# Hybrid decoder trunk: weights of the mixing projections split one step ahead across passes, channel pieces inside the u projection, a late pool stage, and key/value sums in two banks

## The chip, the cores and the metric

The kernel runs on one core of one Trainium2 chip. A core has a matrix engine (PE, which multiplies into eight PSUM banks of 128 x 512 float32), a vector engine (DVE), a scalar engine (ACT), a general engine (POOL), and a queue processor (SP) that here issues nearly all transfers between HBM and the on-chip memory. The metric is the device time of one execution in microseconds (us), the median of the runs shown.

## The reference

Two layers over a sequence of 1024 positions of width 1024, one batch, all in float32. Each layer first mixes tokens and then channels.

```python
h = rms_norm(x, g_pre_mix[l]) * (1.0 + scale_m) + shift_m
proj = h @ w_in[l] + b_in[l]                       # 1024 -> 1280
q, k, v, u = split(proj)                           # 512, 128, 128, 512
attn_out = sliding_window_attention_with_sinks(rotary(q), rotary(k), v, sinks[l])
pool_out = causal_pool_mixer(u, pool_w[l], pool_scale[l])
mix = concatenate([attn_out, pool_out], axis=-1) @ w_out[l]
x = x + gate_m * rms_norm(mix, g_post_mix[l])
h = rms_norm(x, g_pre_ffn[l]) * (1.0 + scale_f) + shift_f
f = (jax.nn.silu(h @ w_gate[l]) * (h @ w_up[l])) @ w_down[l]      # width 2816
x = x + gate_f * rms_norm(f, g_post_ffn[l])
```

Attention has 8 query heads on 2 key/value heads of width 64, a window of 128 and one learned sink per head. The pool mixer takes four groups of 128 channels of u, forms trailing means over 2, 4, 8 and 16 positions minus the token, and multiplies each group by its own 128 x 128 matrix. The six shifts, scales and gates of a layer come from a product of a conditioning vector with `ada_w`.

## The kernel before

**Precision.** Every matmul operand is split into a rounded part hi (ACT, line 213) and the rest lo (DVE, line 214), and each product is three matmuls: hi·hi, hi·lo, lo·hi (lines 239, 242 and 243, function `mm3`). `weight` (216) loads 128 x 512 weights into a staging part called raw and splits them. raw, hi and lo are rings of wide tiles that `part` (124) cuts into pieces of 512 columns: eight pieces of raw, six of hi and six of lo. A new wide tile is only handed out when everything that used the oldest one is done.

**Halves and passes.** The sequence is worked in two halves of 512 positions. The normalised, transposed activations of a half stand in eight tiles hT (one per 128 channels), each holding hi and lo. The input projection of a half is three passes, each over eight steps of 128 channels: `q_pass` (653; four banks of 128 positions x 512), `kv_pass` (617; four banks of which only 256 columns are used, weights of two steps loaded at once, so four steps to the outside), and `u_pass` (674; transposed, four banks of 128 channels x 512 positions). All take their banks from the tag acc, which has four; attention, transposes and the pool product share three banks of the tag msc, and attention's output has one, pv. At the end of a pass the banks are emptied: the query and key/value sums by DVE adds of the bias (lines 672 and 651), the u sums by ACT (line 686).

**Streams.** The passes, attention, the pool mixer and the `ada_w` sums ("side") are Python generators. `run` (596) steps one main stream and, after each of its steps, a share of the others. In a layer the order is: the queries and keys of half 0 (`dense0`, with side); then `dense`, which is u of half 0, keys/values of half 1, queries of half 1, with attention of half 0, the pool mixer of half 0 and side between its 20 steps; then the output projection of half 0 (`mix_out`) with side and attention of half 1; the post-norm of half 0; u of half 1 with ten steps of attention; the channel pieces of half 0 (line 1362); and then `firsts[0]`, the first six jobs of the up product (`up_firsts`, 1002), with the rest of attention and the pool mixer of half 1. A channel piece (`pre_norm_piece`, 494) is four transposes on PE into an msc bank, a scale and shift on ACT into raw (line 475), a store of that to HBM where it is kept for later (line 498), and a split into a tile of hT.

**Weights.** A pass calls `weight` at the start of each step, ahead of that step's matmuls. Only the first queries and keys of layer 0 already split the next step's weights ahead of the current step's matmuls (`first` and `pairs`).

**Order.** The library that turns this program into instructions plans the order on each engine: the order in which the program emits instructions is a priority, and one that is expected to be ready earlier can go out before one emitted ahead of it. Within an engine the instructions then run in the planned order, each waiting on semaphores for what it reads and for the buffer that it writes. This holds for SP's queue of transfers too.

Of the kernel before, what the change touches and what calls it, by code (L numbers as in the profile page):

```python
# [11 lines left out]
F32 = mybir.dt.float32  # L12
# [3 lines left out]
AF = mybir.ActivationFunctionType  # L16
# [49 lines left out]
def hybrid_decoder_kernel(  # L66
# [144 lines left out]
    def split(hi, lo, src):  # L211

        nc.scalar.activation(hi, src, AF.Copy)  # L213
        nc.vector.tensor_sub(lo, src, hi.bitcast(F32))  # L214

    def weight(*srcs):

        raw = part("raw")
        for psl, view, src in srcs:
            dst = raw[psl]  # L220
            if view:
                dst = dst.rearrange("p (a b) -> p a b", a=view)
            nc.sync.dma_start(dst, src)
        hi, lo = part("hi"), part("lo")
        split(hi, lo, raw)
        return hi, lo

    def after(ins, prev):
        tc.add_manual_dep(
            ins.ins, prev.ins.name,  # L230
            mybir.DependencyInfo(mybir.DependencyClass.NoSync, mybir.DependencyReason.DATA),
            reason="order on the same engine",
        )

    ALLP = slice(0, P)
    tiles = [slice(t * P, (t + 1) * P) for t in range(NT)]
# [377 lines left out]
    halos = {}  # L614
    attn = {}

    def kv_pass(l, hT, par, qkvs, pairs=None):

        if pairs:
            dsts = [pairs[t // 2][:, t % 2 * 256 : t % 2 * 256 + 256] for t in range(NT)]  # L620
        else:
            dsts = [acc_bank()[:, :256] for _ in range(NT)]

        def rows(k):
            return weight(
                (ALLP, 2, w_in[l, k * P : (k + 2) * P, ATT:QKV].rearrange("(a p) n -> p a n", p=P))
            )

        ahead = None
        if pairs:  # L630
            ahead = rows(0)
            yield
        for k in range(KD):
            if k % 2 == 0:
                (wh, wl), ahead = ahead or rows(k), None
            elif pairs and k + 1 < KD:
                ahead = rows(k + 1)
            cs = slice(k % 2 * 256, k % 2 * 256 + 256)
            hi, lo = hT[k]
            for t in range(NT):  # L640

                first, second = pairs and t % 2 == 0, pairs and t % 2 == 1
                other = mm3(
                    dsts[t], hi[:, tiles[t]], lo[:, tiles[t]], wh[:, cs], wl[:, cs],
                    k == 0 and not second, k == KD - 1 and not first,
                    other if second and k in (0, KD - 1) else None,
                )
            if k % 2 == 1:
                yield
        for t in range(NT):  # L650
            nc.vector.tensor_add(qkvs[t][:, ATT:QKV], dsts[t], par["bq"][:, ATT:QKV])

    def q_pass(l, hT, par, qkvs, first=False):

        banks = [acc_bank() for _ in range(NT)]

        def rows(k):
            return weight((ALLP, None, w_in[l, k * P : (k + 1) * P, 0:ATT]))

        ahead = None  # L660
        if first:
            ahead = rows(0)
            yield
        for k in range(KD):
            wh, wl = ahead or rows(k)
            ahead = rows(k + 1) if first and k + 1 < KD else None
            hi, lo = hT[k]
            for t in range(NT):
                mm3(banks[t], hi[:, tiles[t]], lo[:, tiles[t]], wh, wl, k == 0, k == KD - 1)
            yield  # L670
        for t in range(NT):
            nc.vector.tensor_add(qkvs[t][:, 0:ATT], banks[t], par["bq"][:, 0:ATT])

    def u_pass(l, h, hT, cols, uts, piece_read):
        banks = [acc_bank() for _ in range(4)]
        for k in range(KD):
            wh, wl = weight((ALLP, None, w_in[l, k * P : (k + 1) * P, QKV:INW]))
            for g in range(4):
                sl = slice(g * P, (g + 1) * P)
                ins = mm3(banks[g], wh[:, sl], wl[:, sl], *hT[k], k == 0, k == KD - 1)  # L680
            piece_read(k, ins)
            yield
        for g in range(4):
            ut = t_("uT", [P, HALO + T])
            c0 = 6 * KD + 2 * KD + 4 + g
            nc.scalar.activation(ut[:, HALO:], banks[g], AF.Identity, bias=cols[:, c0 : c0 + 1])
# [198 lines left out]
            prev = cur  # L885
        flush()

    POOL_STEPS = len(WINDOWS)

    def pool_mix(l, h, uts, cols, cat):  # L890

        raw = part("raw")
        nc.sync.dma_start(raw.rearrange("p (g d) -> p g d", g=4), pool_w[l].rearrange("g c d -> c g d"))
        pwh, pwl = (t_(tag, [P, 512], F32R) for tag in ("pwh", "pwl"))
        split(pwh, pwl, raw)
        for g, w in enumerate(WINDOWS):
# [13 lines left out]
            if h == 0:  # L910
                head = pooled[:, 0:HALO]
                nc.vector.tensor_mul(head, cur[:, HALO : 2 * HALO], rcnt[:, g, :])
                nc.vector.tensor_sub(head, head, u[:, HALO : 2 * HALO])
            hi, lo_ = part("hi"), part("lo")
            split(hi, lo_, pooled)
            bank = msc_bank()
            sl = slice(g * P, (g + 1) * P)
            mm3(bank, pwh[:, sl], pwl[:, sl], hi, lo_, True, True)
            sc = cols[:, 8 * KD + g : 8 * KD + g + 1]
            nc.scalar.activation(cat[:, g, :], bank, AF.Copy, scale=sc)  # L920
            yield

    def mix_out(l, cats, G):
        order = [*range(GRP, KD), *range(GRP)]
# [336 lines left out]
    wss = [ada_first_load(0)]  # L1261
    hts = {0: []}
    qkvs0 = [t_("qkv", [P, QKV]) for _ in range(NT)]
    queries0 = q_pass(0, hts[0], par, qkvs0, True)
    pv = ps.tile([P, 512], F32, tag="pv", name="pv", bufs=1)
    keys0 = kv_pass(0, hts[0], par, qkvs0, (pv, msc_bank()))
    acc = ada_first_row(wss[0])
    normalise(0, xs, stats(xs, t_("rs", [P, 8])), True)
    next(queries0)
    next(keys0)  # L1270
    wss.append(ada_first_load(CW))
    NB0 = D // CW

# [35 lines left out]
    def ada_jobs(l):  # L1309
        return ada_stream(ada_gate(l, 0) + ada_pair(l, 1, par["cols"], par["abf"]))  # L1310

    FIRST = (3, 6)
    for l in range(DEPTH):
# [13 lines left out]
        qkvs[0] = [t_("qkv", [P, QKV]) for _ in range(NT)] if l else qkvs0  # L1327

        def dense0():
            yield from q_pass(l, hts[0], par, qkvs[0]) if l else queries0  # L1330
            yield from kv_pass(l, hts[0], par, qkvs[0]) if l else keys0
# [5 lines left out]
        att = attention(0, qkvs[0], par["nsink"], cats[0][0])  # L1337

        def dense():
            yield from u_pass(l, 0, hts[0], cols, uts[0], piece_read)  # L1340
            yield from kv_pass(l, pieces, par, qkvs[1])
            yield from q_pass(l, pieces, par, qkvs[1])

        def pool0():
            for _ in range(KD):
                yield
            yield from pool_mix(l, 0, uts[0], cols, cats[0][1])

        run(dense(), 2 * KD + 4, (att, ATT_STEPS + 2), (pool0(), 2 * KD + 4), (side, 16))
        drain(att)  # L1350
        cats[1] = (t_("cfb", [P, 4, T]), t_("cfb", [P, 4, T]))
        G = load_gate(l, 0)
# [148 lines left out]
```

## Time and profile before

| | |
|---|---|
| three runs | 1982.2 us median (1977.94 to 1982.73) |
| the profiled execution, its own time | 1979.58 us |
| its span (first to last instruction) | 1977.8 us |
| PE busy | 1891.2 us (96%) |
| weight loads of PE busy | 1551.3 us (78%) |
| DVE busy | 1564.9 us (79%) |
| ACT busy | 957.1 us (48%) |
| POOL busy | 49.7 us (3%) |
| mean granted clock of PE | 0.985 |

Busy times are unions of an engine's instructions; a matmul's end is modelled. The granted clock is the share of the full PE clock that the chip gave. "L651" is line 651 of the kernel before. In names such as `acc<-hi,hT` the tile written stands first, then those read: moving operand, then stationary. A group "PE acc L239 <- ACT hi L213: 4.1, 3, 2.2" says that PE stood idle ahead of matmuls of line 239 into acc until ACT's line 213 had written hi: 4.1 us in total, 3 times, 2.2 us the longest.

### The profile page before, as it was taken

To read this page: it belongs to the slowest core of one execution; us is meant where nothing else is said; L and a number is where in the kernel's file an instruction comes from. 1 tells how busy PE (TensorE), PEld (TensorE's weight loads), DVE (VectorE), ACT (ScalarE), POOL (GpSimd) and SP (SyncE) were. 2 spreads that over 40 slices of the span, in tenths; PEclk is the share of its full clock that TensorE was granted. 3 is DMA by queue.
4 is the path that set the end of the run, shared out by engine and by line. 5 is a ranking of instruction groups with operands and counts; after the bars stand their busy time and mean duration, and the time that the engine had idled before them with its cause. 6 is when DMAs were issued, how large, how long until landed. Compare 5 with 4: busy or idle time off the path is not lost. (4 is left out here: it accounts for less than half of the span.)

```text
span 1977.8 us, 26045 instructions
## 1 busy us (share of the span) xinstructions
PE 1891.2 (96%) x8958; PEld 1551.3 (78%) x8958; DVE 1564.9 (79%) x2907; ACT 957.1 (48%) x1794; POOL 49.7 (3%) x100
## 2 busy tenths in 40 slices
PE   6989989999999999999999899899999999999997
PEld 4877768887888887778887777788778888878886
DVE  6988976679889886787878889656788898767687
ACT  4775785653222223445648658845522222335452
POOL 1000000010000000000000000000200000000000
PEclk9999989999999999999999899899999999999999
DMA  9236553555455446842556455445555554474343
GB/s 327 88 108 187 176 192 121 160 192 192 157 180 192 161 164 229 302 129 88 178 192 182 131 146 184 135 131 189 176 192 176 175 177 170 142 262 171 112 134 112
DMA packets 222052, 336.62 MB, mean 170 GB/s; under 512 B 16696, under 2 KB 120008, under 8 KB 221920
## 3 DMA queue, kind: packets, MB, share of 16 engines
q1 hardware_dynamic: 221776, 334.92, 51.2%
q8 instruction: 70, 1.15, 0.2%
q14 instruction: 62, 0.51, 0.1%
q0 software_dynamic: 32, 0.00, 0.0%
q10 hardware_dynamic: 112, 0.04, 0.0%
HBM read 262.00 MB, written 72.89 MB: 169 GB/s over the span
## 5 line engine op out<-in xcount | busy, mean ns | idle before, releaser
L213 ACT ACTIVATE hi<-raw 128x1024 fp32r<-128x1024 f32 (+1 forms) x388 | 332.0, 867 | 335.7 <-PE acc L242 214.5
L214 DVE TENSOR_TENSOR lo<-raw,hi 128x1024 fp32r<-128x1024 f32 (+1 forms) x388 | 379.7, 984 | 80.6 <-ACT hi L213 77.1
L239 PE MATMUL acc<-t,hi 128*128 128x512 f32 x704 | 276.1, 392 | 4.9 <-ACT hi L213 4.9
L243 PE MATMUL acc<-t,lo 128*128 128x512 f32 x704 | 275.9, 393 | 3.6 <-DVE lo L214 3.6
L242 PE MATMUL acc<-t,hi 128*128 128x512 f32 x704 | 275.5, 391 | 0.0
L243 PE MATMUL acc<-bh,lo 128*128 128x512 f32 x528 | 207.1, 392 | 0.0
L239 PE MATMUL acc<-bh,hi 128*128 128x512 f32 x528 | 203.9, 391 | 3.0 <-ACT bh L213 3.0
L239 PE MATMUL acc<-hT,hi 128*128 128x512 f32 x480 | 192.0, 400 | 9.7 <-ACT hi L213 9.1
L1061 DVE TENSOR_TENSOR fn<-acc,fn 128x512 f32<-128x512 f32 x220 | 150.4, 684 | 50.9 <-PE acc L243 50.1
L242 PE MATMUL acc<-hT,hi 128*128 128x512 f32 x480 | 189.7, 395 | 0.0
L243 PE MATMUL acc<-hT,lo 128*128 128x512 f32 x480 | 187.8, 394 | 0.0
L239 PEld LDWEIGHTS acc<-t,hi 128*128 128x128 f32 x704 | 133.3, 189 | 34.1 <-ACT hi L213 6.5
L243 PEld LDWEIGHTS acc<-t,lo 128*128 128x128 f32 x704 | 133.1, 189 | 34.2 <-DVE lo L214 6.7
L242 PEld LDWEIGHTS acc<-t,hi 128*128 128x128 f32 x704 | 133.2, 189 | 27.8
L242 PE MATMUL acc<-ph,hi 128*128 128x512 f32 x320 | 126.4, 395 | 0.7 <-DVE ph L214 0.6
L239 PEld LDWEIGHTS acc<-bh,hi 128*128 128x128 f32 x528 | 99.4, 189 | 24.8 <-ACT bh L213 3.8
L273 DVE SCALAR_TENSOR_TENSOR ada<-ar,c_act,ada 128x512 f32<-128x512 f32 x140 | 104.4, 746 | 15.9 <-DMA ar<-in_ada_w_dram 14.9
L243 PEld LDWEIGHTS acc<-bh,lo 128*128 128x128 f32 x528 | 100.1, 190 | 20.7
L239 PEld LDWEIGHTS acc<-hT,hi 128*128 128x128 f32 x480 | 91.3, 190 | 29.9 <-ACT hi L213 10.8
L999 ACT ACTIVATE fn<-fn 128x512 f32<-128x512 f32 x44 | 27.8, 633 | 168.4 <-DVE fn L1061 157.9
L243 PEld LDWEIGHTS acc<-hT,lo 128*128 128x128 f32 x480 | 90.7, 189 | 18.7 <-DVE lo L214 0.4
L242 PEld LDWEIGHTS acc<-hT,hi 128*128 128x128 f32 x480 | 91.5, 191 | 17.4
(302 smaller groups left out, 3877.1 us busy)
## 6 DMA issues: line engine op xcount, KB each, us to landing
ar<-in_ada_w_dram SPq DMA_DIRECT2D x160, 256.0 KB
raw<-in_w_gate_dram SPq DMA_DIRECT2D x44, 512.0 KB
raw<-in_w_up_dram SPq DMA_DIRECT2D x44, 512.0 KB
raw<-in_w_in_dram SPq DMA_DIRECT2D x80, 256.0 KB
raw<-keeps SPq DMA_DIRECT2D x40, 512.0 KB
keeps<-fn SPq DMA_DIRECT2D x66, 256.0 KB
two_b<-in_w_down_dram SPq DMA_DIRECT2D x30, 512.0 KB
raw<-keepa SPq DMA_DIRECT2D x25, 512.0 KB
```

What stands on the lines that cost most here:

```text
L213: nc.scalar.activation(hi, src, AF.Copy)
L214: nc.vector.tensor_sub(lo, src, hi.bitcast(F32))
L239: ins = nc.tensor.matmul(dst, lh, rh, start=first, stop=False)
L242: nc.tensor.matmul(dst, lh, rl, start=False, stop=False)
L243: return nc.tensor.matmul(dst, ll, rh, start=False, stop=last)
L273: nc.vector.scalar_tensor_tensor(acc, w, c_act[:, i : i + 1], acc, op0=ALU.mult, op1=ALU.add)
L999: nc.scalar.activation(g, g, AF.Silu)
L1061: nc.vector.tensor_add(halves_of(dst)[m], bank, halves_of(src)[m])
```

## The change

- `one_ahead` takes a list of functions that each load and split one weight. It makes the first at once; each call returns the weight that is held and makes the next. The three passes now call such an `ask` in place of `weight`. One `ask` covers several passes: in layer 0 u, key/value and queries of `dense`; in layer 1 also the queries and keys of half 0 ahead of them. So a pass's first weights are emitted in the last step of the pass ahead of it. The first passes of layer 0 and the u pass of half 1 have one each.
- `kv_pass` puts its four sums of 256 columns into two acc banks (two sums in each), as the first one of layer 0 already did with pv and an msc bank. The first matmul of the pass in a bank opens it for both.
- `pool_mix` multiplies a group one group after its split, so it has five steps; the pool mixer of half 0 is stepped 13 times over the 20 steps of `dense` where it was stepped up to 20 times, so that its groups fall at the 13th to 19th step and not at the 9th to 12th.
- The channel pieces of half 0 are stepped along with the u pass of half 1: nothing after its first three steps, one piece after each of the other five, and the last three behind it.

```diff
+    def one_ahead(makers):
+        makers = iter(makers)
+        held = [next(makers)()]
+        def ask():
+            now_ = held.pop()
+            for make in makers:
+                held.append(make())
+                break
+            return now_
+        return ask
...
-    def kv_pass(l, hT, par, qkvs, pairs=None):
-        if pairs:
-            dsts = [pairs[t // 2][:, t % 2 * 256 : t % 2 * 256 + 256] for t in range(NT)]
-        else:
-            dsts = [acc_bank()[:, :256] for _ in range(NT)]
...
+    def all_rows(rows, l, step=1):
+        return [lambda k=k: rows(l, k) for k in range(0, KD, step)]
+    def kv_pass(l, hT, par, qkvs, ask, pairs=None):
+        banks = pairs or [acc_bank() for _ in range(2)]
+        dsts = [banks[t // 2][:, t % 2 * 256 : t % 2 * 256 + 256] for t in range(NT)]
         for k in range(KD):
             if k % 2 == 0:
-                (wh, wl), ahead = ahead or rows(k), None
-            elif pairs and k + 1 < KD:
-                ahead = rows(k + 1)
+                wh, wl = ask()
...
-                first, second = pairs and t % 2 == 0, pairs and t % 2 == 1
+                first, second = t % 2 == 0, t % 2 == 1
...
-            wh, wl = weight((ALLP, None, w_in[l, k * P : (k + 1) * P, QKV:INW]))
+            wh, wl = ask()
...
-    POOL_STEPS = len(WINDOWS)
+    POOL_STEPS = len(WINDOWS) + 1
...
+        def mapped(g, hi, lo_):
+            bank = msc_bank()
+            sl = slice(g * P, (g + 1) * P)
+            mm3(bank, pwh[:, sl], pwl[:, sl], hi, lo_, True, True)
+            sc = cols[:, 8 * KD + g : 8 * KD + g + 1]
+            nc.scalar.activation(cat[:, g, :], bank, AF.Copy, scale=sc)
+        late = None
         for g, w in enumerate(WINDOWS):
...
             split(hi, lo_, pooled)
-            bank = msc_bank()
-            sl = slice(g * P, (g + 1) * P)
-            mm3(bank, pwh[:, sl], pwl[:, sl], hi, lo_, True, True)
-            sc = cols[:, 8 * KD + g : 8 * KD + g + 1]
-            nc.scalar.activation(cat[:, g, :], bank, AF.Copy, scale=sc)
+            if late:
+                mapped(*late)
+            late = (g, hi, lo_)
             yield
+        mapped(*late)
+        yield
...
+        ask = one_ahead(
+            (all_rows(q_rows, l) + all_rows(kv_rows, l, 2) if l else [])
+            + all_rows(u_rows, l) + all_rows(kv_rows, l, 2) + all_rows(q_rows, l)
+        )
...
-        run(dense(), 2 * KD + 4, (att, ATT_STEPS + 2), (pool0(), 2 * KD + 4), (side, 16))
+        run(dense(), 2 * KD + 4, (att, ATT_STEPS + 2), (pool0(), KD + POOL_STEPS), (side, 16))
...
-        run(u_pass(l, 1, pieces, cols, uts[1], lambda k, ins: None), KD, (att, 10))
+        kept0 = dr.tile([KD, P, T], F32, tag="h0", name="h0", bufs=DEPTH)
+        hts0 = []
+        def first_half():
+            for _ in range(3):
+                yield
+            for k in range(KD):
+                hts0.append(pre_norm_piece(0, k, par["abf"], None, fn, kept0[k]))
+                yield
+        pre = first_half()
+        ask1 = one_ahead(all_rows(u_rows, l))
+        run(u_pass(l, 1, pieces, cols, uts[1], lambda k, ins: None, ask1), KD, (att, 10), (pre, KD))
         pool = pool_mix(l, 1, uts[1], cols, cats[1][1])
-        kept0 = dr.tile([KD, P, T], F32, tag="h0", name="h0", bufs=DEPTH)
-        hts0 = [pre_norm_piece(0, k, par["abf"], None, fn, kept0[k]) for k in range(KD)]
+        drain(pre)
```

More of the change, by code (lines that the diff above doesn't have):

```diff
@@ L615, in hybrid_decoder_kernel, with kv_rows, q_rows, u_rows @@
     attn = {}
-    def kv_pass(l, hT, par, qkvs, pairs=None):
-        if pairs:
-            dsts = [pairs[t // 2][:, t % 2 * 256 : t % 2 * 256 + 256] for t in range(NT)]
-        else:
-            dsts = [acc_bank()[:, :256] for _ in range(NT)]
[L624 to L632, printed above, removed]
+    def kv_rows(l, k):
+        return weight(
+            (ALLP, 2, w_in[l, k * P : (k + 2) * P, ATT:QKV].rearrange("(a p) n -> p a n", p=P))
+        )
+    def q_rows(l, k):
+        return weight((ALLP, None, w_in[l, k * P : (k + 1) * P, 0:ATT]))
+    def u_rows(l, k):
+        return weight((ALLP, None, w_in[l, k * P : (k + 1) * P, QKV:INW]))
+    def all_rows(rows, l, step=1):
[3 more added lines that the diff above has]
+        dsts = [banks[t // 2][:, t % 2 * 256 : t % 2 * 256 + 256] for t in range(NT)]
         for k in range(KD):
             if k % 2 == 0:
-                (wh, wl), ahead = ahead or rows(k), None
-            elif pairs and k + 1 < KD:
-                ahead = rows(k + 1)
+                wh, wl = ask()
             cs = slice(k % 2 * 256, k % 2 * 256 + 256)
@@ L651, in kv_pass, with q_pass @@
             nc.vector.tensor_add(qkvs[t][:, ATT:QKV], dsts[t], par["bq"][:, ATT:QKV])
-    def q_pass(l, hT, par, qkvs, first=False):
+    def q_pass(l, hT, par, qkvs, ask):
         banks = [acc_bank() for _ in range(NT)]
[L657 to L663, printed above, removed]
         for k in range(KD):
-            wh, wl = ahead or rows(k)
-            ahead = rows(k + 1) if first and k + 1 < KD else None
+            wh, wl = ask()
             hi, lo = hT[k]
@@ L672, in q_pass, with u_pass @@
             nc.vector.tensor_add(qkvs[t][:, 0:ATT], banks[t], par["bq"][:, 0:ATT])
-    def u_pass(l, h, hT, cols, uts, piece_read):
+    def u_pass(l, h, hT, cols, uts, piece_read, ask):
         banks = [acc_bank() for _ in range(4)]
         for k in range(KD):
-            wh, wl = weight((ALLP, None, w_in[l, k * P : (k + 1) * P, QKV:INW]))
+            wh, wl = ask()
             for g in range(4):
@@ L1263, in hybrid_decoder_kernel @@
     qkvs0 = [t_("qkv", [P, QKV]) for _ in range(NT)]
-    queries0 = q_pass(0, hts[0], par, qkvs0, True)
     pv = ps.tile([P, 512], F32, tag="pv", name="pv", bufs=1)
-    keys0 = kv_pass(0, hts[0], par, qkvs0, (pv, msc_bank()))
+    kv_banks = (pv, msc_bank())
     acc = ada_first_row(wss[0])
     normalise(0, xs, stats(xs, t_("rs", [P, 8])), True)
-    next(queries0)
-    next(keys0)
+    queries0 = q_pass(0, hts[0], par, qkvs0, one_ahead(all_rows(q_rows, 0)))
+    keys0 = kv_pass(0, hts[0], par, qkvs0, one_ahead(all_rows(kv_rows, 0, 2)), kv_banks)
     wss.append(ada_first_load(CW))
@@ L1329, in dense0 @@
         def dense0():
-            yield from q_pass(l, hts[0], par, qkvs[0]) if l else queries0
-            yield from kv_pass(l, hts[0], par, qkvs[0]) if l else keys0
+            yield from q_pass(l, hts[0], par, qkvs[0], ask) if l else queries0
+            yield from kv_pass(l, hts[0], par, qkvs[0], ask) if l else keys0
+        ask = one_ahead(
+            (all_rows(q_rows, l) + all_rows(kv_rows, l, 2) if l else [])
+            + all_rows(u_rows, l) + all_rows(kv_rows, l, 2) + all_rows(q_rows, l)
+        )
         side = ada_jobs(l)
@@ L1339, in dense @@
         def dense():
-            yield from u_pass(l, 0, hts[0], cols, uts[0], piece_read)
-            yield from kv_pass(l, pieces, par, qkvs[1])
-            yield from q_pass(l, pieces, par, qkvs[1])
+            yield from u_pass(l, 0, hts[0], cols, uts[0], piece_read, ask)
+            yield from kv_pass(l, pieces, par, qkvs[1], ask)
+            yield from q_pass(l, pieces, par, qkvs[1], ask)
         def pool0():
```

## The prediction

> **What bounds the kernel now.** I read the busy time of the engines in three long stretches first.
>
> ```profile
> 66.00:300.00 234.00, 214.25 (x1214) 176.96 (x1213) 202.05 (x581) 171.42 (x419) 5.36 (x21) 0.97 0.48 150
> 300.00:1004.00 704.00, 692.52 (x3057) 566.20 (x3057) 553.17 (x762) 294.76 (x447) 15.51 (x16) 0.99 0.52 174
> 1004.00:1275.00 271.00, 248.46 (x1395) 206.73 (x1395) 225.99 (x631) 182.84 (x444) 8.06 (x27) 0.96 0.53 169
> ```
>
> Columns: stretch, length, busy us of PE, weight load, DVE, ACT and POOL with their instruction counts, granted clock, DMA share, GB/s. The first and third rows are token mixing of layers 0 and 1, the second is layer 0's feed-forward. There PE is busy 692.5 of 704, so nothing is to be had; in the two mixing stretches it is idle 19.8 and 22.5 us and its clock is 0.97 and 0.96. The edit touches only those, so its whole stake is some 42 us of idle time and 18 us of clock (0.03 x 234 + 0.04 x 271). PE is the bound in them too, but not alone: DVE is at 86% and 83%.
>
> Second, the same view by stages: key/value and query pass of the second half (107 to 177 in layer 0, and 1085 to 1127, its part with the stalls, in layer 1), u pass of the second half (from 240.3 and 1218.8), what lies between it and the first matmul of the up product (from 271.5 and 1249.8), and that product's first microseconds.
>
> ```profile
> 107.00:144.00 37.00, 31.03 (x203) 26.67 (x203) 33.21 (x92) 23.43 (x62) 1.20 (x4) 0.95 0.32 100
> 144.00:177.00 33.00, 31.47 (x178) 25.84 (x177) 26.44 (x72) 19.71 (x51) 1.09 (x4) 1.00 0.57 170
> 240.30:271.50 31.20, 29.93 (x167) 25.41 (x166) 25.39 (x89) 27.40 (x75) 0.88 (x5) 1.00 0.40 148
> 271.50:288.10 16.60, 10.44 (x68) 8.21 (x66) 10.86 (x30) 14.70 (x31) 0.33 (x1) 0.88 0.67 213
> 288.10:294.30 6.20, 6.20 (x17) 4.91 (x18) 4.64 (x6) 3.69 (x7) 0.00 (x0) 0.51 0.87 266
> 1085.00:1127.00 42.00, 36.54 (x224) 31.31 (x223) 37.31 (x102) 26.48 (x68) 1.00 (x3) 0.88 0.38 115
> 1218.80:1249.80 31.00, 29.72 (x167) 25.26 (x165) 25.23 (x89) 27.21 (x75) 0.83 (x5) 1.00 0.38 145
> 1249.80:1266.60 16.80, 11.06 (x69) 8.67 (x67) 11.03 (x30) 14.87 (x31) 0.33 (x1) 0.81 0.66 213
> 1266.60:1270.60 4.00, 4.00 (x12) 3.19 (x13) 3.82 (x6) 3.70 (x7) 0.00 (x0) 0.52 0.78 240
> ```
>
> The fourth and eighth rows are the largest holes: 6.2 and 5.7 us idle, and after each the clock is halved (0.51, 0.52). In the key/value part DVE runs at 90% (33.21 of 37).
>
> Third, PE's waits, of layer 0 (four rows) and layer 1 (three): total, times, longest.
>
> ```profile
> PE acc L239 <- ACT hi L213: 4.1, 3, 2.2
> ...
> PE msc L239 <- ACT hi L213: 1.9, 1, 1.9
> ...
> PE acc L239 <- DVE qkv L651: 1.3, 1, 1.3
> ...
> PE acc L242 <- DVE lo L214: 0.7, 1, 0.7
> ```
> ```profile
> PE acc L239 <- ACT hi L213: 5.5, 4, 2.5
> ...
> PE acc L239 <- DVE qkv L672: 1.9, 1, 1.9
> ...
> PE acc L242 <- DVE lo L214: 1.5, 1, 1.5
> PE acc L239 <- DVE qkv L651: 1.4, 1, 1.4
> ```
>
> **The change, part by part.** No arithmetic is added or removed: the same matmuls, splits, adds and transfers are issued at other places.
>
> *Weights split one step ahead.* It can remove PE's waits for a weight's hi and lo. One wait in each layer's hi row is the up product's, not ours:
>
> ```profile
> 288.06 0.80 PE L239 MATMUL acc<-hT,hi 128*128 128x512 f32 x1 [1.70 <-ACT hi L213]
> ```
> ```profile
> 1266.58 0.80 PE L239 MATMUL acc<-hT,hi 128*128 128x512 f32 x1 [1.73 <-ACT hi L213]
> ```
>
> So 4.1 - 1.7 + 0.7 = 3.1 and 5.5 - 1.7 + 1.5 = 5.3, 8.4 us in all. The lower end is nothing, or a loss (the last rival): the order of each engine is planned, and a split may already stand as early as its engine allows.
>
> *Key/value sums in two banks.* The matmuls and the four adds of L651 stay, and the order now fixed between the halves of a bank changes which matmul comes first, not how many: it costs PE nothing. A key/value pass needs only two freed banks (L672), and the query pass behind it finds two of its four banks free, so that half of its first step covers the adds (L651): 1.3 + 1.9 + 1.4 = 4.6 us. Nothing at the lower end.
>
> *Late pool stage.* The four pool groups move from the key/value steps to the query steps, and a group's three matmuls come one group after its split. It meets the 1.9 us wait of the msc bank on a split.
>
> Together 14.9 us of waits. The clock lost beside them is 0.05 x 37 + 0.12 x 42 = 6.9 us. Upper end 21.8. How much of it is real is set by DVE: in 107 to 177 it has 59.65 us of work (33.21 + 26.44), and at the 90% that it reaches in the first of these rows it needs 66.3 of the 70 us, a saving of 3.7 where the waits and clock of that stretch are 1.9 + 1.3 + 0.7 + 1.9 = 5.8. That is 64%; as waits of attention remain between, I take half of 21.8: **11 us**.
>
> *Channel pieces in the u projection.* Eight pieces per layer (each four transposes on PE, one ACT scale, one ACT hi, one DVE lo, one store of 256 KB on SP's queue, nothing on POOL's) stood behind the u pass; five of them now go between its steps 4 to 8, past the u pass's last loads on SP, and three remain behind it. Their ACT price:
>
> ```profile
> L475 ACT ACTIVATE raw<-msc,colp 128x512 f32<-128x512 f32 x8 | 5.8, 790 | 0.0
> L213 ACT ACTIVATE hT<-raw 128x512 fp32r<-128x512 f32 x8 | 4.7, 649 | 0.0
> ```
>
> 1.44 us each, 11.5 of the 14.7 us of ACT in the hole: PE waits there because ACT makes the pieces one after the other. The saving is not the hole's idle time, since ACT is at 88% in the u pass already (27.40 of 31.2). From 240.3 to 288.1 (47.8 us) PE has 40.4 us of work. Packed as well as the u pass is (96%), it takes 42.1: 5.7 us saved. ACT has 42.1 us too, and at its own 88% that is 47.9: nothing saved. Some of ACT's work need not come first (three pieces of the second half of the channels are read only by the product's second job), so I go nearer the PE end: 4 us, and 4 in layer 1 (bounds 0 and 5.3 from its rows, 40.8 / 0.959 against 47.8). The clock lost at the hole: 0.49 x 6.2 = 3.0 and 0.12 of the 10.44 busy us = 1.3 in layer 0; 0.48 x 4 = 1.9 and 0.19 x 11.06 = 2.1 in layer 1; 8.3 together, and I take half, as part of the hole stays: 4.2. This part gives **12 us**; its upper end is 5.7 + 5.3 + 8.3 = 19.3. The first job's operand is late next: its load needs staging that the third and fourth piece share with two weights.
>
> A rule that would take the clock terms away stands in the Trainium skill, "TensorE: Matmul & The Clock Gate", section "HAM oscillation — how this bites in real kernels": the clock drops only where PE idles longer than about 3.4 us at a stretch. By it no term of clock would exist here and the sum would be 7 + 8 us. The trace does not agree: the longest single wait in the rows above is 2.5 us, and the clock stands at 0.51 behind waits of 1.7 us; I go by the rows.
>
> The sum: 1979.6 us (span 1977.8 and 1.8 around it) - 11 - 12 = **1957 us**. The three runs' median is 1982.2, 2.6 above that execution; I leave the figure as the sum gives it.
>
> **The rivals.**
>
> *Pieces ahead of their rows.* A piece can only start when the rows are normalised, and they are ready late:
>
> ```profile
> 258.43 2.19 ACT L463 ACTIVATE fn<-fn,rs 128x1024 f32<-128x1024 f32 x2 [0.23 <-DVE rs L257]
> ```
>
> That ends at 260.6. The u pass reaches the end of its fourth step at 240.3 + 4 x 3.9 (31.2 / 8) = 255.9. If the first piece's transposes stand there in PE's order, all later u matmuls wait behind them, 4.7 us per layer, and the hole shrinks for nothing: this part falls from 12 to 12 - 9.4 = 3, and the time is 1979.6 - 11 - 3 = 1966. For it: PE takes its matmuls in order. Against: the planner knows that the rows come late and may put the transposes later.
>
> *Loads behind stores.* The stores of the pieces are issued before the loads of the weights two steps on. If SP keeps that order, the sixth weight's load goes out after the first piece is scaled: 260.6 + 0.8 = 261.4.
>
> ```profile
> 282.81 0.46 SPq L1012 DMA_DIRECT2D raw<-in_w_up_dram  x1
> ```
> ```profile
> 286.95 1.06 ACT L213 ACTIVATE hi<-raw 128x1024 fp32r<-128x1024 f32 x1 [0.96 <-DMA raw<-in_w_up_dram]
> ```
>
> From that pair a load takes 4.1 us, so the weight is there at 265.5, split at 266.2, wanted at 240.3 + 5 x 3.9 = 259.8: 6.4 us late per layer. The 8 us of idle turn into -4.8 and the clock's 4.2 are lost: 1979.6 - 11 + 4.8 = 1973. Against it:
>
> ```profile
> 231.62 1.75 SPq L223 DMA_DIRECT2D raw<-in_w_in_dram  x4
> ...
> 245.14 4.29 SPq L527 DMA_DIRECT2D x<-fn  x4
> ```
>
> these four loads come later in the program than those stores and went out 13.5 us ahead of them.
>
> *Everything vanishes.* All waits and clock losses go: 21.8 + 19.3 = 41, 1938 us. DVE and ACT would both have to run at 98% or more; little speaks for it.
>
> *Slower: the ring of split weights runs dry.* Hi and lo parts share a ring of six slots with attention and pool. A weight split ahead holds its slot for a second step; where attention and pool take more than four slots within two steps, the next split can start only when the step's matmuls end, and PE waits for at least its 0.65 us. ACT has such waits already, in layer 0:
>
> ```profile
> ACT hi L213 <- PE acc L243: 6.5, 5, 2.0
> ```
>
> At all 40 steps of the two dense runs (8 u, 4 key/value, 8 query per layer) that is 26 us; the 11 us are gone, the 12 remain: 1979.6 + 26 - 12 = 1994. It outweighs those 12 from 18 steps on. Against it: by the emitted order a step takes some two slots (a weight, attention about 0.7, pool about 0.6), so six last nearly three steps.
>
> **How the numbers follow.** Forecast 0.50, pieces ahead of their rows 0.20, loads behind stores 0.10, everything vanishes 0.08, slower 0.12. A change of 0.3% (6 us) is about what this kernel's measurement tells from none: the three runs lie 4.8 us apart. The forecast's own range is 1952 to 1966 (one third to two thirds of the upper ends 21.8 and 19.3); to leave out little more than the slower case it must reach 1938 below and 1980 above. Faster than 0.3%: nearly all of the forecast (0.47), 0.15 and 0.05 of the next two, 0.08, so 0.75; within 0.3%: 0.13, the rest of the first three; slower 0.12.
>
> **What would show it.** In the profile after: the waits on L651 and L672 gone; no wait of 2 us on a weight's split in the u pass; the first up matmul some 44 us behind the u pass's first (47.8 now), with granted clock near 1 in the 6 us behind it. A long wait of the transposes (L489) on the normalised rows inside the u pass shows the first rival; ACT's hi waiting for DMA there the second; ACT's hi waiting for PE in the query passes the last. The prediction is wrong if the stretch up to 300 us loses less than 5 us, or if DVE's work there stretches the passes by what the waits give back.

## The result, and the profile after

The changed kernel takes 1948.99 us (median of 4 runs, 1946.06 to 1953.98) where the kernel before took 1981.39 (4 runs on the same chip, 1977.94 to 1982.73): a ratio of 0.9842, 95% interval 0.9817 to 0.9866. The forecast was 1957, range 1938 to 1980. The profiled execution took 1948.45 us, its span 1946.7.

The first lines of the page after:

```profile
span 1946.7 us, 26047 instructions
...
PE 1876.9 (96%) x8958; PEld 1544.9 (79%) x8958; DVE 1564.9 (80%) x2907; ACT 954.5 (49%) x1794; POOL 50.0 (3%) x100
```

PE's 8958 matmuls are as many as before, and they were busy for 1876.9 us where they took 1891.2. Of the 31.1 us that the span lost, 16.8 are idle time of PE (86.6 us before, 69.8 after) and 14.3 are busy time of the same matmuls. The higher mean clock (0.991 for 0.985) makes some 11.5 of these, an estimate: 1891.2 x (1 - 0.985 / 0.991). Where the other 3 come from is not shown; a matmul's end is modelled.

The places are read best when each stretch is cut at the same matmul in both kernels. The two token-mixing stretches, from the first u matmul of layer 0 (layer 1: the first query matmul) to the first matmul of the up product (seven matmuls of other streams moved out of each), before:

```profile
66.00:288.10 222.10, 202.35 (x1163) 167.14 (x1161) 193.12 (x562) 164.60 (x405) 5.36 (x21) 0.98 0.48 149
1004.30:1266.60 262.30, 239.76 (x1354) 199.58 (x1352) 219.18 (x617) 177.25 (x435) 8.06 (x27) 0.97 0.52 166
```

and after:

```profile
66.30:273.50 207.20, 197.73 (x1156) 164.86 (x1154) 190.87 (x555) 160.28 (x395) 5.73 (x21) 0.99 0.50 159
988.60:1234.60 246.00, 230.58 (x1347) 196.16 (x1346) 215.96 (x608) 174.10 (x425) 8.04 (x26) 0.99 0.55 176
```

Layer 0 loses 14.9 us and layer 1 16.3, all of the gain: from the start to the first cut is 66.0 and 66.3 us, and the two stretches behind the first up matmuls (288.1 to 1004.3 and 1266.6 to the end before; 273.5 to 988.6 and 1234.6 to the end after) add up to 1427.4 and 1427.2. PE's idle time in the mixing falls from 42.3 to 24.9 us.

The stages of the prediction, after: key/value and query pass of the second half of layer 0 in two rows (cut within the query pass), u pass with pieces up to the first up matmul, the first microseconds of that product; then the same of layer 1, with its two passes in one row.

```profile
103.60:139.50 35.90, 34.64 (x250) 31.30 (x249) 32.64 (x101) 28.16 (x75) 2.73 (x9) 1.00 0.48 141
139.50:166.50 27.00, 25.34 (x142) 20.54 (x141) 25.70 (x67) 16.89 (x44) 1.44 (x4) 1.00 0.53 165
232.20:273.50 41.30, 37.56 (x226) 31.98 (x224) 34.54 (x111) 38.54 (x95) 0.87 (x5) 1.00 0.55 194
273.50:280.00 6.50, 6.48 (x40) 5.58 (x41) 5.81 (x17) 6.38 (x18) 0.33 (x1) 1.00 0.62 186
1069.20:1127.00 57.80, 57.42 (x379) 50.78 (x378) 56.58 (x159) 41.81 (x112) 2.33 (x8) 1.00 0.48 145
1193.30:1234.60 41.30, 37.59 (x227) 32.02 (x225) 34.56 (x110) 38.53 (x95) 0.83 (x5) 1.00 0.56 193
1234.60:1240.00 5.40, 5.36 (x23) 4.52 (x24) 3.69 (x10) 3.96 (x14) 0.33 (x1) 0.68 0.76 229
```

The u pass with the pieces takes 41.3 us in both layers (before 47.8 in both; the forecast had some 44). The key/value and query pass of layer 1 take 57.8 us (before 68.5), with PE busy for 57.42 and DVE for 56.58 of them.

PE's waits in the same two stretches, after, layer 0:

```profile
PE msc L821 <- DVE sb L811: 2.8, 3, 1.3
PE msc L744 <- DVE rt L712: 1.6, 1, 1.6
PE acc L256 <- DVE lo L214: 1.2, 2, 0.8
PE acc L253 <- ACT hi L213: 0.7, 2, 0.4
```

and layer 1:

```profile
PE acc L253 <- ACT hi L213: 4.2, 3, 2.6
PE msc L821 <- DVE sb L811: 3.4, 2, 2.1
PE msc L744 <- DVE rt L712: 2.1, 1, 2.1
PE msc L503 <- DMA raw<-n: 1.8, 1, 1.8
...
PE acc L253 <- DVE qkv L677: 0.2, 1, 0.2
```

The old lines 239, 242, 243 are now 253, 256, 257, and 651, 672 are 666, 677. Waits on the key/value adds (L666) are gone and those on the query adds (L677) are 0.2 us. What is left in attention (L821, softmax) and in the rotary embedding of half 1 (L744) is not what the edit touched. The two waits on the rotary sums are 1.6 and 2.1 us; before, layer 0 had 1.3 us there (L739 on L707) and layer 1 none.

### The profile page after: what moved, and what is told of

It is laid out like the page before. It is cut to its first block, busy times and chain, and to the rows that moved or that the text cites. A ratio compares the mean times of both kernels' runs of the same rounds, so it can differ in the third digit from the quotient of the medians.

```text
span 1946.7 us, 26047 instructions
## 1 busy us (share of the span) xinstructions
PE 1876.9 (96%) x8958; PEld 1544.9 (79%) x8958; DVE 1564.9 (80%) x2907; ACT 954.5 (49%) x1794; POOL 50.0 (3%) x100
```

## The experiments

Three theories of where the 32 us come from were open. The first is the prediction's: each part removes the wait that its text names. The second: one part does most of it, and the others find their wait already gone. The third: what was gained is the placing of the work, so that a part has no price of its own. Each part was undone in the changed kernel, and three of them were also done alone. A comparison is with the kernel before on the same chip in the same series.

| run | median us | before beside it | ratio, 95% interval |
|---|---|---|---|
| changed kernel | 1948.99 | 1981.39 | 0.9842 [0.9817, 0.9866] |
| changed kernel, second series | 1947.23 | 1979.25 | 0.9841 [0.9826, 0.9856] |
| without weights ahead | 1944.63 | 1980.74 | 0.9819 [0.9804, 0.9834] |
| the same, second series | 1949.11 | 1979.25 | 0.9850 [0.9836, 0.9865] |
| without the late pool stage | 1956.44 | 1980.74 | 0.9880 [0.9864, 0.9895] |
| without the two banks | 1954.32 | 1980.74 | 0.9876 [0.9854, 0.9897] |
| without pieces in the u pass | 1958.67 | 1980.74 | 0.9901 [0.9872, 0.9929] |
| weights ahead alone | 1973.05 | 1979.25 | 0.9973 [0.9962, 0.9985] |
| pool stage alone | 1964.75 | 1980.86 | 0.9916 [0.9902, 0.9931] |
| two banks alone | 1973.60 | 1980.86 | 0.9956 [0.9942, 0.9971] |
| weights ahead in one u pass only | 1942.23 | 1979.25 | 0.9818 [0.9800, 0.9836] |
| pool stage late, multiplied at once | 1950.92 | 1980.86 | 0.9846 [0.9830, 0.9862] |
| pieces from the u pass's first step | 1957.99 | 1980.86 | 0.9884 [0.9867, 0.9901] |

One kernel in two series can differ by 4.5 us (without weights ahead: 1944.63 and 1949.11), so smaller differences between series tell nothing.

### Weights split as they are used

Every pass of the loop over layers asks for its weight when it needs it; the first passes of layer 0 keep the split ahead, which they had before.

```diff
+    def each(makers):
+        makers = iter(makers)
+        return lambda: next(makers)()
-        ask = one_ahead(
+        ask = each(
-        ask1 = one_ahead(all_rows(u_rows, l))
+        ask1 = each(all_rows(u_rows, l))
```

> The changed kernel (1949 us) with the split of a mixing weight back at the start of its own step; the other three parts stay. Theory 'shares by waits': the part is worth its share of the waits it was charged with (8.4 of 14.9 us) of the 18 us that the key/value, query and u stretches gained, some 8 us: 1957. Rival 'order decides': the split's place ahead of attention in ACT's and DVE's order is nearly all of it: 1963 or more. Rival 'DVE relief': the moved pool stage is nearly all of it and this part is worth 2 us or less: 1951 or below.

It took 1944.63 us, no longer than the changed kernel. So that this is not the series speaking, it was run once more beside the changed kernel:

> The changed kernel without the split ahead, once more: 1944 to 1946 us under the theory, 2 to 5 us below the changed kernel; equal to it within 1.5 us under the rival.

> The changed kernel itself, beside the next three on one chip. Its four runs gave 1949 us, and without the split ahead 1945 us, with intervals that overlap. Theory now: the split ahead does not pay, its waits come back in the output projection: this kernel is 2 to 5 us slower than the one without it. Rival: the two differ by chance of the chip, under 1.5 us here.

There it took 1949.11 against 1947.23, intervals overlapping: with the three other parts in place, splitting ahead is worth 0 within some 4 us. Alone on the kernel before (the three other parts undone) it is worth 5 to 6 us (0.27% by the ratio, 6.2 us by the medians):

> The kernel before with the split ahead alone (four banks, early pool stage, pieces behind the u pass). Prediction's step: 4 to 8 us faster than before (1973 to 1977). Theory that it only moves waits: the first u pass of layer 0 gains its 4 us, later stages give them back, 1978 to 1983. Rival that it pays where DVE is not yet relieved by the other parts: 1970 or less.

So it does gain, and loses that in company. The second series shows where. The stretch from the first u matmul of layer 0 to the first of half 1, changed kernel:

```profile
66.60:234.10 167.50, 161.41 (x932) 133.93 (x930) 156.04 (x445) 121.67 (x301) 6.20 (x16) 0.98 0.49 148
```

and without weights ahead:

```profile
67.50:236.70 169.20, 159.62 (x932) 132.77 (x930) 156.15 (x445) 121.92 (x301) 5.65 (x15) 0.99 0.48 145
```

PE is idle 6.1 us in the first and 9.6 in the second: 3.5 us of waits were taken away. But PE's same 932 matmuls are busy for 161.41 and 159.62 us at clocks of 0.98 and 0.99, and half of the gain is gone. By the starts of the stages, u and key/value pass take 57.6 us with the split ahead and 60.9 without, and the output projection behind them 68.1 and 63.6 (in the first series 57.6 and 60.2, then 65.7 and 64.2). That the output projection is longer is for the most part clock. PE waits for the rotary sums at its start in both kernels, 1.6 us in the changed one and 1.3 without weights ahead. The row in the changed kernel, first series (start, duration, what, idle time before it):

```profile
171.23 0.51 PE L744 MATMUL msc<-ident,hi 128*128 128x128 f32 x4 [1.62 <-DVE rt L712]
```

The stretch with this wait, and the next one, whose clock is halved:

```profile
169.65:173.06 3.41, 1.54 (x8) 1.07 (x8) 3.41 (x15) 2.85 (x7) 0.00 (x0) 1.00 0.48 150
173.06:176.48 3.42, 3.32 (x11) 2.61 (x11) 3.42 (x7) 2.56 (x5) 0.00 (x0) 0.50 0.49 146
```

That costs 1.7 us, and the output projection is 1.5 us longer. Without weights ahead the clock is 1.00 from 168 to 232 us. In the second series it is halved from 172.6 to 179.4 us in the changed kernel, 3.4 us of the 4.5, and not at all in the other (1.00 from 173 to 236.7). Why the rotary wait is 0.3 us longer with the split ahead is not shown.

### Weights ahead in layer 0's first u pass only

In layer 0 the u pass of half 0 keeps the split ahead; all other passes ask for weights as they use them.

```diff
-        ask = one_ahead(
-            (all_rows(q_rows, l) + all_rows(kv_rows, l, 2) if l else [])
-            + all_rows(u_rows, l) + all_rows(kv_rows, l, 2) + all_rows(q_rows, l)
-        )
+        first = all_rows(q_rows, l) + all_rows(kv_rows, l, 2) if l else []
+        ask = each(first + all_rows(kv_rows, l, 2) + all_rows(q_rows, l))
+        ask_u = None if l else one_ahead(all_rows(u_rows, l))
-            yield from u_pass(l, 0, hts[0], cols, uts[0], piece_read, ask)
+            yield from u_pass(l, 0, hts[0], cols, uts[0], piece_read, ask_u or each(all_rows(u_rows, l)))
-        ask1 = one_ahead(all_rows(u_rows, l))
+        ask1 = each(all_rows(u_rows, l))
```

> The changed kernel with the split ahead kept only in the first u pass of layer 0, where PE's waits on splits went (37.3 us for 41.2); key/value, query and the other u passes split in their own step. Theory that the loss sits in the key/value and query passes and the output projection behind them: both gains, 1939 to 1942. Rival that an earlier end of the u pass only shifts attention's work into later stages: no better than without any split ahead, 1944 to 1947.

It took 1942.23 us, the lowest median of all, 5.0 below the changed kernel beside it, but the intervals overlap (0.9800 to 0.9836 and 0.9826 to 0.9856). Its u pass did not keep the gain that it was made to keep (u and key/value pass: 42.8 and 20.2 us, 63.0 in all, where without any split ahead it was 60.9). It is not shown to beat the changed kernel.

### The pool stage where it was

The pool group's matmuls follow its split at once again, and its four groups fall on steps 9 to 12.

```diff
-    POOL_STEPS = len(WINDOWS) + 1
+    POOL_STEPS = len(WINDOWS)
-            if late:
-                mapped(*late)
-            late = (g, hi, lo_)
+            mapped(g, hi, lo_)
             yield
-        mapped(*late)
-        yield
-        run(dense(), 2 * KD + 4, (att, ATT_STEPS + 2), (pool0(), KD + POOL_STEPS), (side, 16))
+        run(dense(), 2 * KD + 4, (att, ATT_STEPS + 2), (pool0(), 2 * KD + 4), (side, 16))
```

> The changed kernel with the pool groups back in the key/value steps (9th to 12th of the 20) and each group's matmuls right behind its split. Theory 'shares by waits': worth 1.9 of 14.9 us of waits plus some of the clock, 3 us: 1952. Rival 'DVE relief': DVE was at 90% in the key/value steps, so taking 14 us of pool work out of them is the main gain: 1960 or more. Rival 'order decides': 1951 or below.

1956.44 us: 7 to 9 us are lost. Alone on the kernel before, the pool stage is worth 16.1 us (1964.75 for 1980.86), the largest of the three parts tried alone:

> The kernel before with the pool part alone (moved and late). Undone from the changed kernel this part cost 7.5 us. If the parts add up it gives the same here: 1971 to 1974. If they overlap, because the pool part and the banks part both free PE from the same crowded DVE queue, it gives more alone: 1970 or less.

The prediction had given it 1.9 us, one wait in an msc bank. What it does stands in DVE's order in the kernel before, at the boundary of the key/value and the query pass of layer 1 (start, duration, instruction; the lines of one pool group are 903, 907, 912 and 913):

```profile
1109.86 0.70 DVE L903 TENSOR_TENSOR pt<-pt 128x525 f32<-128x525 f32 x1
1110.47 0.42 DVE L651 TENSOR_TENSOR qkv<-acc,bqkv 128x256 f32<-128x256 f32 x1
1110.80 0.69 DVE L903 TENSOR_TENSOR pt<-pt 128x521 f32<-128x521 f32 x1
...
1112.41 0.42 DVE L651 TENSOR_TENSOR qkv<-acc,bqkv 128x256 f32<-128x256 f32 x1
1112.74 0.68 DVE L907 SCALAR_TENSOR_TENSOR pt<-pt,uT 128x512 f32<-128x512 f32 x1
...
1114.09 0.68 DVE L214 TENSOR_TENSOR lo<-raw,hi 128x512 fp32r<-128x512 f32 x1
1114.69 0.17 DVE L913 TENSOR_TENSOR pt<-pt,uT 128x16 f32<-128x16 f32 x1
```

DVE is without a gap there. The adds that empty the key/value banks and the low part of the next query weight have to stand in line between the pool's sums. Among the rows left out are also two sums of side (lines 271 and 273, 0.48 and 0.74 us); no run moved these. PE and ACT both wait for DVE here. PE:

```profile
1112.88 0.49 PE L239 MATMUL acc<-hi,hT 128*128 128x512 f32 x1 [1.44 <-DVE qkv L651]
1114.83 0.80 PE L242 MATMUL acc<-lo,hT 128*128 128x512 f32 x1 [1.45 <-DVE lo L214]
```

and ACT, which stands at the pool's split and has the queries' hi parts (line 733) and a softmax behind it:

```profile
1114.89 0.63 ACT L213 ACTIVATE hi<-pt 128x512 fp32r<-128x512 f32 x1 [5.68 <-DVE pt L913]
1115.43 0.40 ACT L733 ACTIVATE hi<-qkv 128x256 fp32r<-128x256 f32 x1
```

With the pool stage alone moved, and the key/value sums still in four banks, PE has no wait on the key/value adds in either layer. These are all its waits in the two passes of layer 1 (kernel with the pool stage alone):

```profile
PE msc L827 <- DVE sb L817: 1.3, 2, 0.6
PE pv L257 <- ACT pth L213: 0.5, 1, 0.5
PE pv L260 <- DVE ph L214: 0.5, 1, 0.5
```

With the pool stage put back and all else changed, the passes of layer 1 take 68.0 us (57.8 in the changed kernel):

```profile
1068.90:1136.90 68.00, 62.20 (x378) 52.76 (x377) 59.92 (x164) 41.94 (x112) 3.17 (x8) 0.95 0.44 133
```

In them ACT stands at the pool's split for 6.5 us at once,

```profile
ACT hi L213 <- DVE pt L926: 6.5, 1, 6.5
```

and PE waits on the key/value adds again, although they are in two banks:

```profile
PE acc L253 <- DVE qkv L666: 1.9, 1, 1.9
```

### Late steps, or late matmuls?

The part has two halves: the groups come at later steps, and each multiplies one group after its split. Here the first stays and the second is undone: as in the last diff, but with 13 steps of 20.

```diff
+        run(dense(), 2 * KD + 4, (att, ATT_STEPS + 2), (pool0(), KD + POOL_STEPS + 1), (side, 16))
```

> The changed kernel with the pool groups at their new place among the query steps, but each group's three matmuls right behind its split again. Theory: the place is what counts, since in the key/value steps ACT's pool split stood waiting for DVE with attention's work behind it (8.0 us of waits before, none after): 1946 to 1950, within 2 us of the changed kernel. Rival: the late matmuls count, as PE's 1.9 us wait on the pool split showed: 1953 or more, as with the whole part undone (1956).

1950.92 us, ratio 0.9846 (changed kernel 0.9841 and 0.9842): the place is what counts. The passes are shorter still (the query pass of layer 1 35.1 us for 37.7), but the output projection behind is longer by more (73.3 for 66.5): work crossed the boundary, and the two together are 4 us longer in layer 1. In layer 0 the end did not move (key/value pass to output projection 128.3 us for 128.6).

### Four banks for the key/value sums

```diff
-        banks = pairs or [acc_bank() for _ in range(2)]
-        dsts = [banks[t // 2][:, t % 2 * 256 : t % 2 * 256 + 256] for t in range(NT)]
+        if pairs:
+            dsts = [pairs[t // 2][:, t % 2 * 256 : t % 2 * 256 + 256] for t in range(NT)]
+        else:
+            dsts = [acc_bank()[:, :256] for _ in range(NT)]
-                first, second = t % 2 == 0, t % 2 == 1
+                first, second = pairs and t % 2 == 0, pairs and t % 2 == 1
```

> The changed kernel with key/value sums in four banks again. Theory 'shares by waits': 4.6 us of waits plus some of the clock that fell behind them, 6 us: 1955, with waits of PE on the key/value and query adds back (1.3, 1.4 and 1.9 us before). Both rivals: 3 us or less, 1952 or below, since with less in DVE's queue the adds come in time for four banks as well.

1954.32 us: some 5 to 7 us lost. The wait on the query adds in layer 1 is back (1.3 us), but no wait on the key/value adds. Of the 4.9 us between this profiled execution and the changed kernel's, only 1.9 lie in the two mixing stretches and 3.2 in layer 0's feed-forward, which the part doesn't touch, so its price beside the others is the least certain. Alone:

> The kernel before with the key/value sums in two banks alone. Undone from the changed kernel this part cost 5.3 us. Adding up: 1973 to 1976. Overlapping with the pool part: 1971 or less. The step of the prediction: 4.6 us of waits and some of the clock behind them, 1973 to 1977.

7.3 us gained. It does remove the wait on the query adds: layer 1's first queries and keys take 33.3 us (35.6 before, 33.7 in the changed kernel), and PE has no wait there. It doesn't remove the wait on the key/value adds; in layer 1's two passes with the banks alone that is PE's only long one (line 670 is the old 651):

```profile
PE acc L257 <- DVE qkv L670: 2.8, 1, 2.8
```

### Pieces behind the u pass

The pieces are no longer stepped with the u pass; all eight are made behind it, as before.

```diff
-        run(u_pass(l, 1, pieces, cols, uts[1], lambda k, ins: None, ask1), KD, (att, 10), (pre, KD))
+        run(u_pass(l, 1, pieces, cols, uts[1], lambda k, ins: None, ask1), KD, (att, 10))
```

> The changed kernel with the channel pieces of the first half behind the u pass again. Theory: the hole between the u pass and the up product comes back in both layers, 6.5 us of length each and a half-clock stretch behind it: 13 to 17 us, 1962 to 1966. Rival 'the hole shrank because of the weights ahead' (the u pass ended earlier and the first operand was loaded earlier): 1955 or below.

1958.67 us: 10 to 12 us are lost, and the hole is back in full, with a clock of 0.62 behind it (layer 0, then layer 1 without the row behind):

```profile
231.40:278.90 47.50, 40.59 (x233) 33.74 (x231) 36.94 (x118) 41.63 (x105) 1.36 (x6) 0.94 0.48 170
278.90:285.00 6.10, 6.03 (x22) 4.88 (x23) 4.70 (x6) 3.80 (x8) 0.00 (x0) 0.62 0.90 268
1198.40:1246.20 47.80, 40.14 (x233) 33.52 (x231) 36.87 (x119) 41.63 (x105) 1.33 (x6) 0.96 0.49 171
```

As this kernel splits its weights ahead and the one without weights ahead still has 41.1 us here, the hole was closed by the pieces and not by the weights.

### Pieces from the first step

The three empty steps ahead of the pieces are taken out, so that the pieces are emitted before their rows can be ready.

```diff
         def first_half():
-            for _ in range(3):
-                yield
             for k in range(KD):
```

> The changed kernel with the channel pieces stepped from the u pass's first step and not its fourth, so that their transposes are emitted well ahead of the normalised rows. The prediction's first rival (transposes stand in PE's order ahead of their rows and hold the u pass up): 4 us or more of PE waits on the normalised rows in each layer, 1955 or more. Theory that the planner places them by when the rows are due: no such wait, the stretch from the u pass to the up product 41 us as now, 1945 to 1950.

1957.99 us, ratio 0.9884: most of this part's gain is lost, 45.6 and 45.2 us for 41.3. But not by waiting for rows. The transposes' groups in the two kernels (count, duration, first and last start), changed kernel first:

```profile
L503 PE MATMUL msc<-ident,fn x32: 270/273/330, 250.4 to 269.3; 128*128 128x128 f32 x32
```

and with the pieces from the first step:

```profile
L503 PE MATMUL msc<-ident,fn x32: 271/273/328, 246.7 to 274.5; 128*128 128x128 f32 x32
```

No transpose waited for rows in either: the planner brought the rows forward and put the transposes behind them. PE stood before a u matmul instead:

```profile
255.46 0.51 PE L253 MATMUL acc<-hT,hi 128*128 128x512 f32 x1 [3.01 <-ACT hi L213]
```

That matmul's weight was split by ACT here, without idle time of ACT before it:

```profile
254.78 0.63 ACT L213 ACTIVATE hi<-raw 128x512 fp32r<-128x512 f32 x1
```

ACT had pieces and a softmax ahead of it, but its order isn't what PE waited for: the weight itself was late. Its load stood in SP's queue behind the stores of two pieces, and SP waited 6.8 us for ACT to make the first of them:

```profile
SPq L512 <- ACT raw L489: 7.9, 4, 6.8
```
```profile
249.50 0.99 SPq L512 DMA_DIRECT2D h<-raw  x2
251.53 0.33 SPq L223 DMA_DIRECT2D raw<-in_w_in_dram  x1
```

By the trace's record of that transfer it landed at 254.53, 0.25 us ahead of the split, while PE had been idle since 252.45. Layer 1 has the same wait (3.02 us; landed 1219.34, split 1219.90). The loads of the pass's last four weights go out 20.3 to 24.4 us into it; in the changed kernel the last two go out at 11.0 and 11.4 us and the others ahead of the pass. The three empty steps are worth some 8 us, of which the two waits make 6: they keep the weights' loads ahead of the pieces' stores on SP's queue.

### The parts together

Undone one at a time they cost about 0, 8, 6 and 11 us: 25 of the 32. Three alone gain 6, 16 and 7, and with 11 for the pieces that makes 40. Neither adds up, because pool, banks and weights ahead relieve the same passes. From the first matmul of the second half's key/value pass to the first of the output projection, the profiled executions lose 7.7 and 7.6 us (layers 0 and 1) with the pool stage alone, 2.3 and 2.3 with the banks alone and 2.3 and 2.6 with the weights alone: 24.8 in all. The changed kernel loses 7.0 and 10.5 there, 17.5. So the second theory fits these three, with the pool stage as the part that does most, and the first fits the pieces. That the three meet in DVE's queue is seen at the one boundary above; elsewhere it is argued.

## Why the prediction was right, and where it was not

The kernel gained 32 us where 23 were forecast. The time is 8 us below the forecast, inside the range (1938 to 1980), and 3 us below the forecast's own range (1952 to 1966). The main mechanisms were right: two mixing stretches and nothing else, waits of PE there, the hole in front of the up product and the clock behind it.

**"Channel pieces in the u projection", 12 us: right.** Undoing them costs 10 to 12. The stage lost 6.4 us per layer and not 4. ACT ran at 93% of it (38.54 of 41.3) and not at 88%, and 3.6 us of its work (42.10 before) left the stage, which is the "some of ACT's work need not come first" of the text; in layer 0 nobody waited for it: PE was busy for 6.48 of the 6.5 us behind it, at the full clock. The clock behind the hole gave back more than the half that was taken: 1.00 and 0.68 where it had been 0.51 and 0.52.

**"So much of it is real is set by DVE", half of 21.8: wrong.** This is the step that cost the 8 us. I took the 90% that DVE reached in the kernel before for what it can reach. It ran at 98% of layer 1's passes (56.58 of 57.80) and at 93% in layer 0's (58.34 of 62.9). With 32 less 12 us, weights, banks and pool together are worth some 20 and not 11; with the whole 21.8 in place of half of it the sum would have been 1946. The 90% was no limit of the engine, only what was left of a stretch that had stalls in it. Nor were the 5.8 us all that could go there: layer 0's passes lost 7.1, as waits of attention that the sum left out fell too (2.9 us in 107 to 177 before, 1.6 after).

**The shares within these 21.8: wrong in order.** The prediction had 8.4 for the weights, 4.6 for the banks, 1.9 for the pool stage; alone they gain 6, 7 and 16 us. I costed the pool stage by the one wait of PE that names its bank, and charged the waits on the key/value adds to the banks and that on the low part to the weights. At the boundary in layer 1 both stood behind the pool's sums on DVE: with the pool stage alone no wait on the adds is left there, nor in layer 0, and with the banks alone it is 2.8 us. The row that would have told it, ACT's 5.68 us wait on the pool's sums, was in the trace of before, in the largest of ACT's waits from 1035 to 1130 us (8.0 us, 3 times). The sum charged PE's waits only, and not what the engines that PE waits for were waiting for.

**"Weights split one step ahead": its low end.** The bounds were nothing and 8.4 us. In the changed kernel it is worth nothing within some 4 us. It takes waits away in the passes, as forecast, and most of what the output projection gives back is clock, for which the sum had no loss.

**The clock.** Terms of 6.9 and 8.3 us were put up, and half of each taken. The mean clock gave some 11.5 us, three quarters of the 15.2. Idle time lost 16.8 of the 25.9 that the bounds 14.9, 5.7 and 5.3 held.

**The rivals.** *Pieces ahead of their rows* didn't come: the first transposes ran 18.2 us behind the start of the u pass without a wait. Nor did they wait where the pieces were emitted from the first step. *Loads behind stores* didn't come in the changed kernel, but it did with the pieces from the first step: a weight was late there by 3.0 us per layer where the rival had 6.4, and some 8 us were lost where it had 16 (1973 for 1957). SP, changed kernel (the first piece's store is the last row, the u weights' loads the first):

```profile
243.19 0.81 SPq L223 DMA_DIRECT2D raw<-in_w_in_dram  x2
...
253.49 0.33 SPq L512 DMA_DIRECT2D h<-raw  x1
```

*The ring runs dry* didn't come: ACT's waits of a split on PE in the mixing, changed kernel, layer 0:

```profile
ACT hi L213 <- PE acc L257: 7.1, 6, 2.3
```

where 6.5 us in 5 times stood before, and the rival needed 0.65 us more at every step. *Everything vanishes* (1938) was nearer than I held likely: no run reached it, the lowest median is 1942.23.

**"What would show it".** The waits on L651 are gone and those on L672 all but gone (0.2 us). The first up matmul comes 41.3 us behind the u pass's first, better than 44; the clock behind it is 1.00 in layer 0, but 0.68 in layer 1. One sign failed: layer 1's u pass of half 0 still has a wait of 2.6 us on a weight's split (1022.3 to 1069.2, 46.9 us long, 45.5 before), in spite of the split ahead. The trace shows where: the weight had landed at 1037.1 us, but ACT worked without a gap from 1034.97 to 1041.47, on pieces, a softmax and a table load of 1.28 us, before it split it. Why the planned order puts the split behind these is not shown.

## What to carry to other kernels

Where PE waits for an engine, read what that engine itself was waiting for and what stood ahead in its order, before a wait is charged to the part of the edit that names its buffer: here waits under three names (the adds' banks, a weight's low part, ACT's split) had one cause, a chain of sums on DVE at the boundary of two passes. A busy share read from a stretch with stalls in it is no ceiling for the engine. And work that is moved into a busy pass must be placed behind that pass's own preparation on each engine and queue that it uses: three empty steps ahead of the pieces, which keep the weights' loads ahead of the pieces' stores, were worth 8 us.

## What the runs showed of the hardware

The granted clock fell behind short waits throughout. In the traces of this case it is 1.00 or 0.50, and 0.50 lasts 3.41 us or two or three times that. Cut into pieces of this length, the changed kernel shows in layer 1:

```profile
1040.05:1043.46 3.41, 1.32 (x10) 1.16 (x11) 2.48 (x8) 3.23 (x10) 0.00 (x0) 1.00 0.22 65
1043.46:1046.87 3.41, 3.41 (x17) 3.11 (x16) 3.21 (x9) 2.13 (x4) 0.00 (x0) 0.50 0.68 184
```

PE is idle for 2.1 us of the first piece, in the wait of 2.6 us on a weight's split, and the next piece runs at half clock. Over the fourteen profiled executions, cut at this grid from 30 to 1930 us, each fall to 0.50 came behind a piece in which PE was idle for 1.4 to 2.9 us in sum. A piece with more than 1.95 us was never followed by 1.00; between 1.4 and 1.95 both occurred. In the Trainium skill, "TensorE: Matmul & The Clock Gate", the section "HAM oscillation — how this bites in real kernels" has the clock drop only behind idle times above some 3.4 us; the longest wait from 1022.3 to 1047 is 2.6 us, so the trace does not agree. A later section of that page, "A second HAM failure mode: psum-queue depth-cycling", tells of frequent short idle times between groups of matmuls that make the clock swing; that is nearer to these rows, but no run here took such waits one by one.

That removing 17 us of scattered waits also gave back some 11 us of clock is the larger surprise: the clock stood at 0.50 for 60.9 us before and for 38.2 in the changed kernel, and half of the difference is lost time. By this a microsecond of short waits cost some 1.7 here. A single piece at 0.50 costs 1.7 us, so two kernels that lie a few us apart may differ by one or two of them.

The Trainium skill's "Perfetto Trace Analysis", section "Tensor Engine Instruction (MATMUL, LD_WEIGHTS)", calls ACT and DVE strictly first in, first out. ACT's rows above agree: for 5.68 us it stood at one split, and the instruction of line 733 that followed had no semaphore of its own to wait for.
